# A bidirectional hybrid encoder layer on one core: the first four output blocks computed four rows of input at a time

## The chip, the core and the metric

The kernel runs on one core of a Trainium2 chip. The core has a matrix engine (TensorE, PE in the profile; its weight loads are shown as PEld), a vector engine (VectorE, DVE), a scalar engine (ScalarE, ACT), GpSimd (POOL, unused here but for four constants) and SyncE (SP), whose queue issues almost all transfers from HBM into on-chip memory (SBUF). TensorE writes its sums to PSUM, which here is cut into four accumulators named g and four named s. The metric is the device time of one launch in microseconds (us); the kernel before takes 1975.64 us (median of 3 runs, 1975.63 to 1977.07).

## What is computed

One encoder layer on 256 tokens of width 2048: a root-mean-square norm, one wide projection, a latent attention branch, a two-directional state-space branch, a gated sum, and a feed-forward block. Only the start of it matters here:

```python
n = rms_norm(h, norm_mix_w[l])
u = n @ w_in[l]
q_lat, kv_lat, k_rope, z, xbc, dt_f, dt_b, g_attn, g_ssd = jnp.split(u, IN_SPLITS, axis=-1)
# q_lat and kv_lat are 512 wide each; each is normed again:
q = (rms_norm(q_lat, q_norm_w) @ w_uq)
kv = (rms_norm(kv_lat, kv_norm_w) @ w_ukv)
```

The rest of `u`, the two branches and the feed-forward block follow, and the output is normed once more. All of it is float32.

## The kernel before

**Tiles.** Activations lie transposed: channels on the 128 partitions, the 256 tokens along the row. x is 16 blocks of 128 channels, called k = 0 to 15, and is loaded as four tiles x0 to x3 of four blocks each (512 KB). A weight is cut into blocks of 128 output channels; one such block has 16 sub-blocks of 128x128, one for each k, and is loaded into a tile `raw` (1024 KB). There are three `raw` buffers (`RAWB`).

**Split arithmetic.** A float32 weight w is split into wh (ScalarE copies it to the rounded type fp32r, line 150) and wl = w - wh (VectorE, line 151), eight sub-blocks at a time: a "half". There are five buffers (`HB`) for wh and five for wl, so at most five halves are split ahead. x times the norm's weight is called xw (VectorE, line 275) and is split in the same way into xHL, which holds the high part and the low part side by side (ScalarE line 281, VectorE line 282). One sub-block then costs TensorE two instructions: wh times both parts (512 columns, line 176) and wl times the high part (256 columns, line 177).

**Jobs.** The program is a list of jobs, each one block of outputs: job 0 to 3 give q_lat, 4 to 7 kv_lat, and so on through the layer. Job i takes one accumulator g, runs over its 16 k, and is then evacuated: ScalarE copies one half of g to SBUF and VectorE adds the other (`halves_sum`, lines 228 and 229). An accumulator is free again when both have read it; there are four. For each half that TensorE takes, the loop at the end of the program loads raw tiles and splits halves up to `HB` ahead (`load`, `split_to`).

**The first job.** Job 0 uses no split: it multiplies float32 weights with float32 xw (`first_slab`, line 1143), all 16 k into one accumulator, while the xHL tiles are made.

**Side work.** Slots hang other work on a job: at slot 2 the squares of x (`emit_xsq`: four squares of 1024 columns on ScalarE, three sums of 1024 columns on VectorE and a last one of 512 columns, tiles xsq and xacc), at slot 4 the sums of these over channels on TensorE (line 243, accumulators s).

**What sets the order.** Inside the part marked `manual_schedule` the written order stands. Elsewhere a planner places each engine's instructions by its own costs; an engine then executes its queue strictly in that order. SP's queue issues a transfer only when an earlier transfer on the same one of eight counters has landed.

Of the kernel before, what the change touches and what calls it, by code (L numbers as in the profile page):

```python
# [15 lines left out]
P = 128  # L16
S = 256
# [30 lines left out]
class Job:  # L48


    def __init__(self, src, nb, mm, evac):
        self.src, self.nb, self.mm, self.evac = src, nb, mm, evac
        self.sides, self.post = [], []
        self.whole = None
        self.quad = False


@with_exitstack
def tile_bidir_hybrid_layer(ctx: ExitStack, tc, xT, pos, vec, cst, w_in, w_r, w_v, w_qk, w_oa,
                            w_os, w_out, w_up, w_dn, out, RAWB=3, HB=5, NPG=29, NP1=18):  # L60
    nc = tc.nc
# [7 lines left out]
    act, dve, pe = nc.scalar, nc.vector, nc.tensor  # L69

    def page(shape, dt=F32, name="pg"):
        return pp.tile(shape, dt, tag="pg", bufs=NPG, name=name)

    def p1(shape=(P, S), dt=F32, name="p1"):
        return pp.tile(list(shape), dt, tag="p1", bufs=NP1, name=name)

    def gpsum(shape):
        return gps.tile(shape, F32, tag="g", name="g")

    def spsum(shape):  # L80
        return sps.tile(shape, F32, tag="s", name="s")

    def f32(ap):
        return ap.bitcast(F32)


    V = cp.tile([P, NVEC], F32, name="V")
    CT = cp.tile([P, NCONST], F32, name="CT")
    nc.scalar.dma_start(V[:, :16], vec[:, :16])
    xpg = []  # L90

    def load_x(q):
        t = page([P, 4, S], name=f"x{q}")
        nc.sync.dma_start(t, xT[:, 4 * q:4 * q + 4, :])
        xpg.append(t)
# [6 lines left out]
    def vcol(name, i=0):  # L102
        o = VOFF[name] + i
        return V[:, o:o + 1]
# [4 lines left out]
    jobs = []  # L109
    raws = {}  # L110
    halves = []

    def load(i):
        if i >= len(jobs) or i in raws:
            return
        j = jobs[i]
        t = wp.tile([P, 16, P], F32, tag="raw", bufs=RAWB, name="raw")
        raws[i] = t
        if i == 0:

            for h in range(2):
                load_x(2 * h)
                nc.sync.dma_start(t[:, 8 * h:8 * h + 8, :], j.src[:, 8 * h:8 * h + 8, :])
                load_x(2 * h + 1)
        elif i == 1:
            for h in range(2):
                nc.sync.dma_start(t[:, 8 * h:8 * h + 8, :], j.src[:, 8 * h:8 * h + 8, :])
        elif j.quad:
            tq = t.rearrange("p (m k) c -> p m k c", m=4)
            for m, src in enumerate(j.src):  # L130
                nc.sync.dma_start(tq[:, m], src)
        else:
            nc.sync.dma_start(t[:, :j.nb, :], j.src)
# [4 lines left out]
    def split_to(n):  # L138
        while hptr[0] < min(n, len(halves)):
            i, h, nb = halves[hptr[0]]  # L140
            wh = wp.tile([P, 8, P], F32R, tag="wh", bufs=HB, name="wh")
            wl = wp.tile([P, 8, P], F32R, tag="wl", bufs=HB, name="wl")
            if jobs[i].quad:

                r = raws[i].rearrange("p (m k) c -> p m k c", m=4)[:, :, 2 * h:2 * h + 2, :]
                vh, vl = (w.rearrange("p (k m) c -> p m k c", k=2) for w in (wh, wl))
            else:
                r = raws[i][:, 8 * h:8 * h + nb, :]
                vh, vl = wh[:, :nb, :], wl[:, :nb, :]
            act.activation(vh, r, AF.Copy)  # L150
            dve.tensor_sub(vl, r, f32(vh))  # L151
            hl[hptr[0]] = (wh, wl)
            hptr[0] += 1
# [6 lines left out]
    def dense(src, nb, get, evac, cell=None, k0=0, ktot=None, merge=True):  # L160

        cell = {} if cell is None else cell
        ktot = nb if ktot is None else ktot

        def mm(h, n, wh, wl):
            if k0 == 0 and h == 0:
                cell["ps"] = gpsum([P, 2, S] if merge else [P, S])  # L170
            ps = cell["ps"]
            for b in range(n):
                k = k0 + 8 * h + b
                x = get(k)
                if merge:
                    pe.matmul(ps, lhsT=wh[:, b, :], rhs=x, start=k == 0, stop=False)  # L176
                    pe.matmul(ps[:, 0, :], lhsT=wl[:, b, :], rhs=x[:, 0, :], start=False, stop=k == ktot - 1)  # L177
                else:
                    mm3(ps, wh[:, b, :], wl[:, b, :], x[:, 0, :], x[:, 1, :], k == 0, k == ktot - 1)

        def ev():
            if k0 + nb == ktot:
                evac(cell["ps"])
        j = Job(src, nb, mm, ev)
        jobs.append(j)
        return j
# [40 lines left out]
    def halves_sum(ps, o):  # L227
        act.activation(o, ps[:, 1, :], AF.Copy)
        dve.tensor_add(o, o, ps[:, 0, :])  # L229
# [40 lines left out]
    nHL, xHL, r_x, xw = {}, {}, {}, {}  # L270

    def emit_xw(q):
        xw[q] = page([P, 4, S], name="xw")
        for k in range(4):
            dve.tensor_scalar(xw[q][:, k, :], xpg[q][:, k, :], vcol("nmix", 4 * q + k), None, ALU.mult)

    def emit_split(q, st):
        for b in range(2):
            t = page([P, 2, 2, S], F32R, name="xHL")
            v = xw[q][:, 2 * b:2 * b + 2, :]  # L280
            act.activation(t[:, 0], v, AF.Copy)
            dve.tensor_sub(t[:, 1], v, f32(t[:, 0]))
            st[2 * q + b] = t
# [24 lines left out]
    def pair(st, k):  # L308
        return st[k // 2][:, :, k % 2, :]
# [70 lines left out]
    def lat_evac(which, m):  # L380
        def ev(ps):
            if m == 0:
                lat[which] = page([P, 4, S], name=which)
                lat[which + "s"] = p1(name=which + "s")
            sq = lat[which + "s"] if m == 0 else p1(name="sq1")
            o = lat[which][:, m, :]
            if len(ps.shape) == 2:
                act.activation(o, ps, AF.Copy)
            else:
                halves_sum(ps, o)  # L390
            act.activation(sq, o, AF.Square)
            if m:
                dve.tensor_add(lat[which + "s"], lat[which + "s"], sq)
        return ev
# [565 lines left out]
    win_i = [0]  # L960

    def win(evac, st=nHL, merge=True):
        j = dense(w_in[win_i[0]], 16, lambda k: pair(st, k), evac, merge=merge)
        win_i[0] += 1
        return j
# [3 lines left out]
    def at(slot, fn, *a):  # L969
        late.append((slot, lambda: fn(*a)))  # L970

    for m in range(4):
        win(lat_evac("q", m), xHL, m > 0)
    for m in range(4):
        win(lat_evac("kv", m), xHL, True)
    win(kr_evac)
# [99 lines left out]
    for g in range(G):  # L1076
        b = len(jobs)
# [21 lines left out]
    b = len(jobs)  # L1099
# [4 lines left out]
    b = len(jobs)  # L1104
# [5 lines left out]
    b = len(jobs)  # L1110
# [9 lines left out]
    b = len(jobs)  # L1120
    parts = ((0, 16), (16, 32), (32, 44))
    di = 0
    for pi, (m0, m1) in enumerate(parts):
# [3 lines left out]
        n = m1 - m0  # L1127
# [8 lines left out]
    for s, fn in late:  # L1136
        jobs[s].sides.append(fn)
    base = []

    def first_slab():  # L1140
        ps = gpsum([P, S])
        for k in range(16):
            pe.matmul(ps, lhsT=raws[0][:, k, :], rhs=xw[k // 4][:, k % 4, :], start=k == 0, stop=k == 15)
        return ps
    jobs[0].whole = first_slab
    for i, j in enumerate(jobs):
        base.append(len(halves))
        if j.whole:
# [2 lines left out]
            halves.append((i, h, min(8, j.nb - 8 * h)))  # L1151
    for i in range(RAWB):
        load(i)
    nc.sync.dma_start(CT, cst)
    nc.sync.dma_start(V[:, 16:], vec[:, 16:])

    warm = spsum([P, P])
    for i in range(13):
        pe.matmul(warm, lhsT=ones, rhs=ones, start=True, stop=True)
    with tc.manual_schedule():  # L1160
        emit_xw(0)
        emit_xw(1)
        emit_split(0, xHL)
        emit_xw(2)
        emit_split(1, xHL)
        emit_xw(3)
        emit_split(2, xHL)
        split_to(1)
        emit_split(3, xHL)
        split_to(2)  # L1170
    for i, j in enumerate(jobs):
        load(i + RAWB - 1)
        for fn in j.sides:
            fn()
        if j.whole:
            ps = j.whole()
            raws.pop(i, None)
            lat_evac("q", 0)(ps)
            continue
        for h in range((j.nb + 7) // 8):  # L1180
            n = base[i] + h
            k = halves[min(n + HB - 1, len(halves) - 1)][0]
            for q in range(i, k + 1):
                load(q)
            split_to(n + HB)
            wh, wl = hl.pop(n)
            j.mm(h, halves[n][2], wh, wl)
        raws.pop(i, None)
        for fn in j.post:
            fn()  # L1190
        j.evac()
# [88 lines left out]
```

## Time and profile before

| what | value |
|---|---|
| runs | 1975.63, 1975.64, 1977.07 us; median 1975.64 |
| the profiled execution's own time | 1974.66 us |
| its span, first to last instruction | 1972.9 us |
| granted TensorE clock, mean | 0.998 |
| HBM read | 371.91 MB |

The views used are the page (busy time of each engine), the waits (which engine waited for which line, and for how long), the timeline (single instructions of one engine in order of time), groups of instructions by line, the transfers with their time from issue to landing, and a table by stretches of time (windows), whose columns are busy time and count for each engine, then the granted TensorE clock, the share of time in which the 16 transfer engines were busy, and GB/s. In the timeline a row holds the start, the time, the engine, the line and the tiles, and in brackets the idle time ahead of it and what ended it.

### The profile page before, as it was taken

To read this page: it belongs to the slowest core of one execution; us is meant where nothing else is said; L and a number is where in the kernel's file an instruction comes from. 1 tells how busy PE (TensorE), PEld (TensorE's weight loads), DVE (VectorE), ACT (ScalarE), POOL (GpSimd) and SP (SyncE) were. 2 spreads that over 40 slices of the span, in tenths; PEclk is the share of its full clock that TensorE was granted. 3 is DMA by queue.
4 is the path that set the end of the run, shared out by engine and by line. 5 is a ranking of instruction groups with operands and counts; after the bars stand their busy time and mean duration, and the time that the engine had idled before them with its cause. 6 is when DMAs were issued, how large, how long until landed. Compare 5 with 4: busy or idle time off the path is not lost.

```text
span 1972.9 us, 29057 instructions
## 1 busy us (share of the span) xinstructions
PE 1956.5 (99%) x11136; PEld 1702.4 (86%) x11136; DVE 1466.5 (74%) x2349; ACT 1208.5 (61%) x1892; POOL 0.2 (0%) x4
## 2 busy tenths in 40 slices
PE   9999999999999999999999999999999999999997
PEld 8899988888888888888888888888888888888886
DVE  7997745779887988888455576888657777557776
ACT  6666544688988898786444455555435555345564
POOL 0000000000000000000000000000000000000000
PEclk9999999999999999999999999999999999999999
DMA  7554456666466556645766565555555555555553
GB/s 289 166 175 157 137 180 225 230 214 220 165 215 214 204 180 220 221 158 173 229 198 200 199 219 192 188 188 186 185 192 186 180 190 192 179 185 192 187 161 123
DMA packets 93260, 379.32 MB, mean 192 GB/s; under 512 B 10688, under 2 KB 11328, under 8 KB 62912
## 3 DMA queue, kind: packets, MB, share of 16 engines
q1 hardware_dynamic: 91440, 375.09, 56.2%
q10 hardware_dynamic: 1680, 2.37, 0.4%
q8 instruction: 87, 1.43, 0.3%
q14 instruction: 53, 0.43, 0.1%
HBM read 371.91 MB, written 4.33 MB: 191 GB/s over the span
## 4 chain that ended last, share of the span: by engine, by line
PE 93%; DVE 3%; ACT 2%; issue 1%; DMA 1%; SPq 0%; DVEq 0%; ACTq 0%
PE g L176 41%; PE g L177 21%; PE g L204 7%; PE g L206 7%; PE g L205 7%; PE g L158 1%; PE g L157 1%; PE g L156 1%; DVE wl L151 1%; ACT wh L150 1%; PE s L780 1%; PE s L157 0%; PE s L789 0%; DVE bcf L675 0%; PE s L158 0%
## 5 line engine op out<-in xcount | busy, mean ns | idle before, releaser
L151 DVE TENSOR_TENSOR wl<-raw,wh 128x1024 fp32r<-128x1024 f32 (+1 forms) x670 | 809.3, 1212 | 393.9 <-ACT wh L150 381.5
L150 ACT ACTIVATE wh<-raw 128x1024 fp32r<-128x1024 f32 (+1 forms) x670 | 700.3, 1048 | 647.8 <-PE g L176 433.1
L176 PE MATMUL g<-xHL,wh 128*128 128x512 f32 x1424 | 503.7, 398 | 2.0 <-DVE cu L229 2.0
L176 PE MATMUL g<-hHL,wh 128*128 128x512 f32 x1360 | 477.6, 396 | 0.0
L177 PE MATMUL g<-xHL,wl 128*128 128x256 f32 x1424 | 399.8, 281 | 0.8 <-DVE wl L151 0.8
L177 PE MATMUL g<-hHL,wl 128*128 128x256 f32 x1360 | 381.6, 281 | 0.0
L176 PEld LDWEIGHTS g<-xHL,wh 128*128 128x128 f32 x1424 | 267.3, 188 | 65.7 <-issue 1.2
L176 PEld LDWEIGHTS g<-hHL,wh 128*128 128x128 f32 x1360 | 255.1, 188 | 60.8
L177 PEld LDWEIGHTS g<-xHL,wl 128*128 128x128 f32 x1424 | 269.1, 189 | 1.5 <-DVE wl L151 1.1
L177 PEld LDWEIGHTS g<-hHL,wl 128*128 128x128 f32 x1360 | 257.0, 189 | 0.0
L176 PE MATMUL g<-aHL,wh 128*128 128x512 f32 x692 | 243.7, 398 | 0.0
L177 PE MATMUL g<-aHL,wl 128*128 128x256 f32 x692 | 193.2, 280 | 0.0
L176 PEld LDWEIGHTS g<-aHL,wh 128*128 128x128 f32 x692 | 130.0, 188 | 32.1 <-DVE aHL L919 0.7
L177 PEld LDWEIGHTS g<-aHL,wl 128*128 128x128 f32 x692 | 130.5, 189 | 0.1
L204 PE MATMUL g<-wh,xHL 128*128 128x512 f32 x256 | 100.1, 392 | 0.0
L204 PE MATMUL g<-wh,yHL 128*128 128x512 f32 x256 | 99.8, 390 | 0.0
L206 PE MATMUL g<-wh,xHL 128*128 128x512 f32 x256 | 99.8, 390 | 0.0
L205 PE MATMUL g<-wl,xHL 128*128 128x512 f32 x256 | 99.8, 390 | 0.0
L206 PE MATMUL g<-wh,yHL 128*128 128x512 f32 x256 | 99.6, 389 | 0.0
L205 PE MATMUL g<-wl,yHL 128*128 128x512 f32 x256 | 99.6, 389 | 0.0
L901 DVE SCALAR_TENSOR_TENSOR uc<-u,V,uc 128x255 f32<-128x255 f32 x176 | 84.7, 481 | 4.6 <-ACT uc L899 1.5
L176 PE MATMUL g<-mHL,wh 128*128 128x512 f32 x240 | 83.6, 392 | 0.0
(298 smaller groups left out, 2603.5 us busy)
## 6 DMA issues: line engine op xcount, KB each, us to landing
raw<-in_w_in SPq DMA_DIRECT2D x88, 1024.0 KB, 4.9
raw<-in_w_up SPq DMA_DIRECT2D x88, 1024.0 KB, 4.9
raw<-in_w_in SPq DMA_DIRECT2D x128, 256.0 KB, 4.0
raw<-in_w_os SPq DMA_DIRECT2D x128, 256.0 KB, 3.5
raw<-in_w_dn SPq DMA_DIRECT2D x32, 1024.0 KB, 4.9
raw<-in_w_oa SPq DMA_DIRECT2D x64, 256.0 KB, 3.8
FB<-acsD SPq DMA_DIRECT2D x32, 512.0 KB, 7.5
raw<-in_w_out SPq DMA_DIRECT2D x14, 1024.0 KB, 4.9
```

What stands on the lines that cost most here:

```text
L150: act.activation(vh, r, AF.Copy)
L151: dve.tensor_sub(vl, r, f32(vh))
L156: pe.matmul(ps, lhsT=wH, rhs=xH, start=first, stop=False)
L157: pe.matmul(ps, lhsT=wH, rhs=xL, start=False, stop=False)
L158: pe.matmul(ps, lhsT=wL, rhs=xH, start=False, stop=last)
L176: pe.matmul(ps, lhsT=wh[:, b, :], rhs=x, start=k == 0, stop=False)
L177: pe.matmul(ps[:, 0, :], lhsT=wl[:, b, :], rhs=x[:, 0, :], start=False, stop=k == ktot - 1)
L204: pe.matmul(ps, lhsT=x[:, 0, ts], rhs=wH[:, kk, :], start=k == 0, stop=False)
L205: pe.matmul(ps, lhsT=x[:, 0, ts], rhs=wL[:, kk, :], start=False, stop=False)
L206: pe.matmul(ps, lhsT=x[:, 1, ts], rhs=wH[:, kk, :], start=False, stop=k == kt - 1)
L780: pe.matmul(px[j0][:, b, c * P:(c + 1) * P], lhsT=q.xw[:, 1 - c, js], rhs=q.cX[:, 1 - c, :], start=True, stop=True)
L901: dve.scalar_tensor_tensor(o[:, a], u[:, b], vcol("fcw", k * 88 + cb), o[:, a], ALU.mult, ALU.add)
```

## The change

Jobs 0 to 3 no longer are one output block each. They become four units: unit u holds sub-blocks k = 4u to 4u+3 of all four q_lat blocks. All four accumulators g are taken by unit 0 and are kept until unit 3 is done; then all four are evacuated. Unit 0 (k = 0 to 3) multiplies in float32 without a split; units 1 to 3 use the split. A unit's raw tile is loaded in four pieces of 256 KB (rows of 2 KB in each partition) in place of one or two transfers with rows of 8 or 4 KB. At k = 4 the instruction with wh is issued as two of 256 columns. The tiles x0 to x3 are loaded one ahead of each unit's raw tile, the small tile V (the norm's weights) goes first on SP's queue in place of ScalarE's, the split of x0 is made last, and ten rather than thirteen warm-up matmuls are issued.

```diff
-    nc.scalar.dma_start(V[:, :16], vec[:, :16])
+    nc.sync.dma_start(V[:, :16], vec[:, :16])
...
-        if i == 0:
...
-            for h in range(2):
-                load_x(2 * h)
-                nc.sync.dma_start(t[:, 8 * h:8 * h + 8, :], j.src[:, 8 * h:8 * h + 8, :])
-                load_x(2 * h + 1)
-        elif i == 1:
...
+        if j.four:
...
+            if i < 3:
+                load_x(i)
+            for m, src in enumerate(j.src):
+                nc.sync.dma_start(t[:, 4 * m:4 * m + 4, :], src)
...
-    for m in range(4):
-        win(lat_evac("q", m), xHL, m > 0)
...
+    lps = []
+
+    def first_unit(u):
+        def mm(h, n, wh, wl):
+            for b in range(8):
+                m, k = 2 * h + b // 4, 4 * u + b % 4
+                x = pair(xHL, k)
+                if k == 4:
+                    for i in range(2):
+                        pe.matmul(lps[m][:, i, :], lhsT=wh[:, b, :], rhs=x[:, i, :], start=False, stop=False)
+                else:
+                    pe.matmul(lps[m], lhsT=wh[:, b, :], rhs=x, start=False, stop=False)
+                pe.matmul(lps[m][:, 0, :], lhsT=wl[:, b, :], rhs=x[:, 0, :], start=False, stop=k == 15)
+
+        def whole():
+            for m in range(4):
+                lps.append(gpsum([P, 2, S]))
+                for k in range(4):
+                    pe.matmul(lps[m][:, 0, :], lhsT=raws[0][:, 4 * m + k, :], rhs=xw[0][:, k, :],
+                              start=k == 0, stop=False)
+
+        def ev():
+            if u == 3:
+                for m in range(4):
+                    lat_evac("q", m)(lps[m])
+        j = Job([w_in[m][:, 4 * u:4 * u + 4, :] for m in range(4)], 16, mm, ev)
+        j.four = True
...
+    for u in range(4):
+        jobs.append(first_unit(u))
...
+    load_x(3)
     nc.sync.dma_start(CT, cst)
     nc.sync.dma_start(V[:, 16:], vec[:, 16:])
...
-    for i in range(13):
+    for i in range(10):
         pe.matmul(warm, lhsT=ones, rhs=ones, start=True, stop=True)
     with tc.manual_schedule():
         emit_xw(0)
-        emit_xw(1)
+        for q in (1, 2):
+            emit_xw(q)
+            emit_split(q, xHL)
+            split_to(2 * q)
+        emit_xw(3)
+        emit_split(3, xHL)
         emit_split(0, xHL)
...
```

Three queues show what this moves. Numbers behind a tile's name tell its copies apart. Line numbers of the changed kernel are three lower up to the new function.

**SP's queue, from its start.** Before, the raw tiles of jobs 0 to 3 are raw_89, raw_100, raw_103 and raw_197:

```order
L94 DMA x0_90<-in_xT 128x1024
L123 DMA raw_89<-in_w_in 128x1024
L94 DMA x1_93<-in_xT 128x1024
L94 DMA x2_95<-in_xT 128x1024
L123 DMA raw_89<-in_w_in 128x1024
L94 DMA x3_98<-in_xT 128x1024
L127 DMA raw_100<-in_w_in 128x1024 x2
L133 DMA raw_103<-in_w_in 128x2048
L1154 DMA CT_73<-in_cst 128x386
L1155 DMA V_72<-in_vec 128x746
L133 DMA raw_197<-in_w_in 128x2048
```

Now the raw tiles of units 0 to 3 are raw_89, raw_96, raw_103 and raw_208, and raw_257 and raw_311 belong to the first two kv_lat jobs:

```order
L89 DMA V_72<-in_vec 128x16
L94 DMA x0_90<-in_xT 128x1024
L124 DMA raw_89<-in_w_in 128x512 x4
L94 DMA x1_97<-in_xT 128x1024
L124 DMA raw_96<-in_w_in 128x512 x4
L94 DMA x2_104<-in_xT 128x1024
L124 DMA raw_103<-in_w_in 128x512 x4
L94 DMA x3_110<-in_xT 128x1024
L1179 DMA CT_73<-in_cst 128x386
L1180 DMA V_72<-in_vec 128x746
L124 DMA raw_208<-in_w_in 128x512 x4
```

The same bytes come up to the fourth raw tile. x1 now stands behind all of the first raw tile, not behind half of it, and the fourth raw tile ends behind 16 small pieces.

**ScalarE's queue where the fourth raw tile arrives.** Before, with raw_197 of job 3 split as wh_207 and wh_228:

```order
L287 ACTIVATE xacc_255<-x0_90 128x1024
L290 ACTIVATE xsq_257<-x1_93 128x1024
L150 ACTIVATE wh_207<-raw_197 128x1024
L150 ACTIVATE wh_228<-raw_197 128x1024
L228 ACTIVATE q_193<-g_211 128x256
L290 ACTIVATE xsq_260<-x2_95 128x1024
L290 ACTIVATE xsq_263<-x3_98 128x1024
L391 ACTIVATE sq1_248<-q_193 128x256
L150 ACTIVATE wh_267<-raw_253 128x1024
L150 ACTIVATE wh_288<-raw_253 128x1024
L228 ACTIVATE q_193<-g_271 128x256
```

Now, from the second half of unit 3 (wh_235, from the last two pieces of raw_208) on; wh_271 is the first half of job 4:

```order
L147 ACTIVATE wh_235<-raw_208 128x1024
L278 ACTIVATE xHL_175<-xw_170 128x512
L278 ACTIVATE xHL_178<-xw_170 128x512
L278 ACTIVATE xHL_181<-xw_127 128x512
L278 ACTIVATE xHL_184<-xw_127 128x512
L284 ACTIVATE xacc_259<-x0_90 128x1024
L287 ACTIVATE xsq_261<-x1_97 128x1024
L287 ACTIVATE xsq_264<-x2_104 128x1024
L287 ACTIVATE xsq_267<-x3_110 128x1024
L147 ACTIVATE wh_271<-raw_257 128x1024
L147 ACTIVATE wh_291<-raw_257 128x1024
L147 ACTIVATE wh_313<-raw_311 128x1024
```

All of the splits of x3 and x0 and the four squares now stand between the last half of unit 3 and the first half of job 4.

**VectorE's queue up to the evacuation of the q_lat blocks.** Before, g_211 and g_271 are the accumulators of jobs 1 and 2, wl_268 and wl_289 are the two halves of job 4 (raw_253):

```order
L151 TENSOR_TENSOR wl_208<-raw_197,wh_207 128x1024
L151 TENSOR_TENSOR wl_229<-raw_197,wh_228 128x1024
L229 TENSOR_TENSOR q_193<-q_193,g_211 128x256
L291 TENSOR_TENSOR xacc_255<-xacc_255,xsq_260 128x1024
L393 TENSOR_TENSOR qs_194<-qs_194,sq1_248 128x256
L291 TENSOR_TENSOR xacc_255<-xacc_255,xsq_263 128x1024
L151 TENSOR_TENSOR wl_268<-raw_253,wh_267 128x1024
L292 TENSOR_TENSOR xacc_255<-xacc_255 128x512
L151 TENSOR_TENSOR wl_289<-raw_253,wh_288 128x1024
L229 TENSOR_TENSOR q_193<-q_193,g_271 128x256
L151 TENSOR_TENSOR wl_316<-raw_313,wh_315 128x1024
```

Now g_188, g_193, g_198 and g_203 are the four accumulators of the units, and wl_272 to wl_334 belong to jobs 4 and 5:

```order
L288 TENSOR_TENSOR xacc_259<-xacc_259,xsq_264 128x1024
L148 TENSOR_TENSOR wl_272<-raw_257,wh_271 128x1024
L288 TENSOR_TENSOR xacc_259<-xacc_259,xsq_267 128x1024
L148 TENSOR_TENSOR wl_292<-raw_257,wh_291 128x1024
L289 TENSOR_TENSOR xacc_259<-xacc_259 128x512
L148 TENSOR_TENSOR wl_314<-raw_311,wh_313 128x1024
L148 TENSOR_TENSOR wl_334<-raw_311,wh_333 128x1024
L226 TENSOR_TENSOR q_353<-q_353,g_188 128x256
L226 TENSOR_TENSOR q_353<-q_353,g_193 128x256
L226 TENSOR_TENSOR q_353<-q_353,g_198 128x256
L226 TENSOR_TENSOR q_353<-q_353,g_203 128x256
```

The add that frees an accumulator stood behind the halves of the job being computed, one add for each block; now the first of the four adds stands behind all four halves of jobs 4 and 5. Job 4 takes its accumulator from these four.

More of the change, by code (lines that the diff above doesn't have):

```diff
@@ L54, in __init__ @@
         self.whole = None
-        self.quad = False
+        self.quad = self.four = False
 @with_exitstack
@@ L118, in load @@
         raws[i] = t
-        if i == 0:
-            for h in range(2):
-                load_x(2 * h)
-                nc.sync.dma_start(t[:, 8 * h:8 * h + 8, :], j.src[:, 8 * h:8 * h + 8, :])
-                load_x(2 * h + 1)
-        elif i == 1:
-            for h in range(2):
-                nc.sync.dma_start(t[:, 8 * h:8 * h + 8, :], j.src[:, 8 * h:8 * h + 8, :])
+        if j.four:
[3 more added lines that the diff above has]
+                nc.sync.dma_start(t[:, 4 * m:4 * m + 4, :], src)
         elif j.quad:
@@ L970, in at @@
         late.append((slot, lambda: fn(*a)))
-    for m in range(4):
-        win(lat_evac("q", m), xHL, m > 0)
+    lps = []
[22 more added lines that the diff above has]
+        j.four = True
+        if u == 0:
+            j.whole = whole
+        return j
+    for u in range(4):
+        jobs.append(first_unit(u))
+    win_i[0] += 4
     for m in range(4):
@@ L1138, in tile_bidir_hybrid_layer @@
     base = []
[L1140 to L1145, printed above, removed]
     for i, j in enumerate(jobs):
@@ L1161, in tile_bidir_hybrid_layer @@
         emit_xw(0)
-        emit_xw(1)
-        emit_split(0, xHL)
[L1164 to L1170, printed above, removed]
+        for q in (1, 2):
[4 more added lines that the diff above has]
+        emit_split(3, xHL)
+        emit_split(0, xHL)
     for i, j in enumerate(jobs):
@@ L1175, in tile_bidir_hybrid_layer @@
         if j.whole:
-            ps = j.whole()
+            j.whole()
             raws.pop(i, None)
-            lat_evac("q", 0)(ps)
             continue
```

## The prediction

> **What bounds the kernel now.** I read the page first, then TensorE's waits, then the head in the timeline.
>
> ```profile
> span 1972.9 us, 29057 instructions
> PE 1956.5 (99%) x11136; PEld 1702.4 (86%) x11136; DVE 1466.5 (74%) x2349; ACT 1208.5 (61%) x1892; POOL 0.2 (0%) x4
> ```
>
> TensorE is the bound: 1956.5 of 1972.9 us. The launch ends when its work is done, so only its idle time and its rate can change.
>
> ```profile
> PE g L176 <- DVE cu L229: 2.0, 2, 1.1
> PE s L1159 <- DVE epsc L100: 1.0, 1, 1.0
> PE g L1143 <- DVE xw L275: 1.0, 2, 0.7
> ...
> PE g L177 <- DVE wl L151: 0.8, 1, 0.8
> ```
>
> The longest wait is 1.1 us. Nothing between the first split job and the end has slack in which a delay could vanish: what the head loses or gains moves the end. The head itself:
>
> ```profile
> 7.92 1.14 DVE L275 TENSOR_SCALAR xw<-x,V 128x256 f32<-128x256 f32 x4 [1.24 <-DMA x<-in_xT]
> ...
> 16.04 0.39 PE L177 MATMUL g<-xHL,wl 128*128 128x256 f32 x1 [0.76 <-DVE wl L151]
> ...
> 32.87 0.95 PE L243 MATMUL s<-ones,xacc 128*128 128x1 f32 x8
> 33.68 0.48 PE L176 MATMUL g<-xHL,wh 128*128 128x512 f32 x1
> ```
>
> From 16.04 us TensorE runs without a pause. At 33.68 it begins job 4, the first kv_lat block, with jobs 0 to 3 done. From job 4 on both kernels do the same work in the same order, so I compare the start of job 4.
>
> **The start of job 4 after the change.** The order shows that job 4 needs the accumulator g_188, and VectorE's add that frees it now stands behind wl_272, a sum xacc, wl_292, the last xacc, wl_314 and wl_334. wl_272 needs wh_271, and ScalarE makes that only behind wh_235, four splits and four squares. wh_235 needs the last two pieces of the fourth raw tile. So this is a chain of three terms: landing, ScalarE, VectorE. All three are work that lay beside TensorE before, because each accumulator had been freed long ahead of its next use.
>
> ScalarE and VectorE, in rows that show how closely such instructions follow each other:
>
> ```profile
> 18.72 1.05 ACT L150 ACTIVATE wh<-raw 128x1024 fp32r<-128x1024 f32 x1
> 19.68 1.04 ACT L287 ACTIVATE xacc<-x 128x1024 f32<-128x1024 f32 x1
> ...
> 21.57 1.99 ACT L150 ACTIVATE wh<-raw 128x1024 fp32r<-128x1024 f32 x2
> ...
> 23.73 2.00 ACT L290 ACTIVATE xsq<-x 128x1024 f32<-128x1024 f32 x2
> ...
> 46.92 1.66 ACT L281 ACTIVATE xHL<-xw 128x512 fp32r<-128x512 f32 x3
> ...
> 22.84 2.35 DVE L151 TENSOR_TENSOR wl<-raw,wh 128x1024 fp32r<-128x1024 f32 x2
> 25.11 0.41 DVE L229 TENSOR_TENSOR q<-q,g 128x256 f32<-128x256 f32 x1
> 25.44 1.22 DVE L291 TENSOR_TENSOR xacc<-xacc,xsq 128x1024 f32<-128x1024 f32 x1
> ...
> 29.18 0.69 DVE L292 TENSOR_TENSOR xacc<-xacc 128x512 f32<-128x512 f32 x1
> ```
>
> Two wh take 1.99 us where one takes 1.05, so they follow each other 0.94 apart; squares 0.96 (2.00 less 1.04); three splits of 512 columns take 1.66, or 0.55 each. ScalarE: 0.94 (wh_235) + 4 x 0.55 + 4 x 0.96 + 1.05 (wh_271 in full) = 8.0 us. On VectorE 1024-column instructions stand 1.13 apart (2.35 less 1.22); I take 0.60 for the 512-column one (0.69 less the same 0.09): wl_272, xacc, wl_292, the last xacc, wl_314, wl_334 and the add take 1.13 + 1.13 + 1.13 + 0.60 + 1.13 + 1.13 + 0.41 = 6.7 us. This is 14.7 us from landing to free accumulator.
>
> The landing:
>
> ```profile
> 0.73 0.41 ACTq L89 DMA_DIRECT2D V<-in_vec  x1
> ...
> 14.86 24.54 SPq L133 DMA_DIRECT2D raw<-in_w_in  x7
> ...
> raw<-in_w_in SPq DMA_DIRECT2D x1, 1024.0 KB, 6.5
> ...
> 7.00:9.00 2.00, 2.00 (x11) 1.74 (x10) 1.08 (x5) 0.78 (x2) 0.00 (x0) 1.00 1.04 420
> ...
> ...
> 58.29 1.75 SPq L131 DMA_DIRECT2D raw<-in_w_in  x4
> ...
> 60.00:62.00 2.00, 2.00 (x13) 1.75 (x12) 2.00 (x4) 1.83 (x3) 0.00 (x0) 1.00 0.98 314
> ```
>
> The fourth raw tile is issued at 14.86 and lands 6.5 us later, at 21.4. The bytes up to it are the same after the change and the queue stays full (its issue waits for wl_148, about 15 us, while earlier bytes are still on the way). Two things delay it: V's issue ahead of x0 (0.4 us, the first row), and rows of 2 KB. While 4 KB rows arrive the engines move 420 GB/s (7 to 9 us); while the 2 KB rows of a later unit arrive, issued from 58.29 in four pieces, 314 GB/s at a share of 0.98 (60 to 62 us). 256 KB at these rates are 0.62 and 0.83 us: 0.21 us more for each of 16 pieces, at most 3.4 us. The lower end is nothing, since the slow stretch is one unit's short burst and the head's queue is long. I take the middle, 1.7 us: landing at 21.4 + 0.4 + 1.7 = 23.5, between 21.8 and 25.2. Job 4 starts at 23.5 + 14.7 = 38.2, or 4.5 us later than 33.7.
>
> [...]
>
> **What this costs beyond the wait.** Units 1 to 3 end near 32 us (they start near 14 and hold 48 pairs, and jobs 1 to 3 took 16.0 to 32.9 for the same 48). Then TensorE has some 6 us with only the four small L243 matmuls in them. What such a pause does is seen at the kernel's end:
>
> ```profile
> 1960.51 0.28 PE L158 MATMUL g<-aHL,wl 128*128 128x256 f32 x1
> 1960.63 0.50 PE L243 MATMUL s<-ones,ssf 128*128 128x1 f32 x4
> 1961.76 0.61 PE L243 MATMUL s<-ones,sqf 128*128 128x1 f32 x4 [0.62 <-ACT sqf L940]
> ...
> 1962.00:1964.00 2.00, 1.07 (x8) 0.80 (x7) 0.66 (x4) 0.66 (x3) 0.00 (x0) 1.00 0.00 0
> 1964.00:1966.00 2.00, 0.00 (x0) 0.00 (x0) 2.00 (x4) 0.00 (x0) 0.00 (x0) 0.56 0.21 77
> ```
>
> After the last dense matmul at 1960.5 only a few small ones follow, and by 1964.3 the granted clock is halved (0.56 is the mean of 1964 to 1966). So the pause ahead of job 4 halves it too. What a restart takes is seen at the start, in the warm-up matmuls alone:
>
> ```profile
> 1.00:2.00 1.00, 0.96 (x4) 0.96 (x5) 1.00 0.50 57
> 2.00:3.00 1.00, 1.00 (x7) 1.00 (x6) 1.00 0.44 153
> 3.00:4.00 1.00, 1.00 (x7) 1.00 (x7) 1.00 0.89 321
> 4.00:5.00 1.00, 1.00 (x6) 1.00 (x6) 1.00 0.89 317
> 5.00:6.00 1.00, 1.00 (x10) 0.88 (x8) 1.00 1.03 369
> ```
>
> From 1.04 to 5 us there are 4 to 7 records in each us, then 10: half rate for 3.9 us (the clock column shows no value of its own there). Job 4 would run its first 3.9 us at about half rate and lose 3.9 x 0.47 = 1.85 us. Bounds: nothing, if the clock stays up, and 3.2 us, if the slow phase lasts nearly twice as long.
>
> [...]
>
> **Parts that I cost at nothing.** The float32 unit has the same 16 matmuls as job 0; k = 4 adds four instructions of 256 columns; three warm-up matmuls go; the earlier start of unit 1 (below) gains nothing. All lie ahead of the 6 us pause; if that went, the four instructions would cost about 0.4 us. SP's ten more issues lie on an idle queue. The wait is new for everything behind it on TensorE; ScalarE and VectorE meanwhile split up to five halves ahead, so nothing else is late when job 4 starts.
>
> **Sum.** 4.5 + 1.85 = 6.35 us later. The profiled execution took 1974.66 us (span 1972.9 and 1.8 around it): 1981.0. The median shown is 1.0 us above that execution: 1975.64 + 6.35 = 1982.0.
>
> **Rivals.** 0.2% is 3.95 us, about what a measurement of this kernel can tell from no change.
>
> B, small rows at the slow rate throughout: landing 25.2, job 4 at 39.9, +6.2 and +1.85: 1983.7; with the long slow phase 1985.0. For it: the 314 GB/s row. Against: that queue was short.
>
> C, row size costs nothing: landing 21.8, job 4 at 36.5, +2.8 and +1.85: 1980.3.
>
> D, the clock is not halved: +4.5, 1980.1; with C +2.8, 1978.4, within 0.2%. Against: the tail's row, which was halved after a shorter pause.
>
> E, not slower: x1 lands by 9.9 us (two more 256 KB pieces ahead of it than the 7.92 row shows, and V), the split of x1 and of the first half of unit 1 ends near 14.1, and TensorE starts it 1.9 us ahead of the 16.04 row. If the accumulators were free in time this would stay: 1973.7. That needs the fourth raw tile by 33.7 - 1.9 - 14.7 = 17.1 us, and the same bytes needed 21.4. Only an error in my reading of the queues gives this.
>
> **Chances.** Forecast 0.52 (own range 1980.3 to 1983.7), B 0.16, C 0.14, D 0.13, E 0.05. Slower by over 0.2%: the forecast, B, 0.11 of C and 0.08 of D, together 0.87. The remaining 0.13, E and the rest of C and D, lie within 0.2%, but for 0.02 that I leave for an E larger than worked out: 0.11 and 0.02. The range goes from D with C, 1978.4, to B with the long slow phase, 1985.0; this leaves out E and little else.
>
> **What would show it.** Right: TensorE's longest waits stand ahead of the small s matmuls and job 4's first matmul, ended by VectorE's xacc and q lines, some 6 us in all; the granted clock is near 0.5 in a stretch from about 36 to 41 us; job 4 starts near 38; the fourth raw tile lands near 23.5; later waits are as before. Wrong: job 4 by 34, no drop of the clock, or new waits later in the layer.

## The result and the profile after

The changed kernel takes 1982.12 us (median of 6 runs, 1980.53 to 1983.68) where the kernel before took 1975.64 us beside it (6 runs, 1974.53 to 1977.07). The ratio is 1.0033, 95% interval 1.0023 to 1.0043: slower by a third of a per cent. The profiled execution of the changed kernel took 1981.58 us, 6.9 us more than that of the kernel before.

The page of the changed kernel, its span and busy times:

```profile
span 1979.8 us, 29075 instructions
PE 1959.0 (99%) x11134; PEld 1704.6 (86%) x11134; DVE 1466.8 (74%) x2350; ACT 1208.1 (61%) x1892; POOL 0.2 (0%) x4
```

TensorE is busy 2.5 us longer, although it has two instructions less, and idle 4.4 us longer (20.8 us of its span, 16.4 before). Both parts have to be found. First the idle part: TensorE's waits over the whole run (in total, times, longest).

```profile
PE s L240 <- DVE xacc L289: 3.5, 1, 3.5
PE g L173 <- DVE cu L226: 2.0, 2, 1.0
PE g L989 <- DVE xw L272: 1.4, 1, 1.4
...
PE g L173 <- DVE q L226: 0.8, 1, 0.8
```

The first and the last row are new: one wait for VectorE's last sum of squares (xacc), one for its add that frees an accumulator (q). The rows between stood there before, the xw row with 1.0. Where the two lie, TensorE's timeline of the changed kernel shows, with the first matmul of unit 1 that needs a wl, the last one of unit 3, the small s matmuls and job 4's first:

```profile
14.86 0.39 PE L983 MATMUL g<-xHL,wl 128*128 128x256 f32 x1 [0.76 <-DVE wl L148]
...
31.59 0.28 PE L983 MATMUL g<-xHL,wl 128*128 128x256 f32 x1
35.34 1.86 PE L240 MATMUL s<-ones,xacc 128*128 128x1 f32 x8 [3.47 <-DVE xacc L289]
38.03 0.76 PE L173 MATMUL g<-xHL,wh 128*128 128x512 f32 x1 [0.83 <-DVE q L226]
```

Unit 3 is done at 31.87, a microsecond ahead of the place of job 3 before. Then TensorE does nothing but the small s matmuls for 6.2 us. Job 4 begins at 38.03, where it began at 33.68: 4.35 us later. Its first matmul now takes 0.76 us, not 0.48.

The second part is in the stretches of the changed kernel (busy time and count by engine, granted clock, transfers):

```profile
34.00:36.00 2.00, 0.66 (x4) 0.67 (x4) 2.00 (x3) 2.00 (x5) 0.00 (x0) 0.75 0.42 61
36.00:38.00 2.00, 1.20 (x6) 1.12 (x7) 2.00 (x4) 0.09 (x2) 0.00 (x0) 0.50 0.74 307
38.00:41.00 3.00, 2.97 (x9) 2.61 (x10) 2.68 (x6) 2.97 (x7) 0.00 (x0) 0.50 0.93 287
41.00:42.00 1.00, 1.00 (x5) 0.80 (x5) 0.48 (x2) 0.03 (x1) 0.00 (x0) 0.58 0.87 369
```

The clock is halved from 35.0 (0.75 is the mean of one fast and one slow microsecond) to 41.8 (0.58 is slow for 0.84 of a microsecond; from 42 on it is 1.00). This slow stretch of 6.8 us begins inside the pause and covers the first 3.8 us of job 4.

To see what the head costs in all, I follow one VectorE instruction that stands well behind it, in the attention branch, and which both kernels have. Its row in the kernel before, then in the changed kernel:

```profile
134.34 0.16 DVE L610 TENSOR_SCALAR sm<-sm 128x2 f32<-128x2 f32 x1
...
140.35 0.16 DVE L607 TENSOR_SCALAR sm<-sm 128x2 f32<-128x2 f32 x1
```

It is 6.01 us later: 4.35 from the start of job 4, and 1.66 that job 4 lost at half clock. From there to 1917 us the difference stays between 5.4 and 6.1; over the last 50 us it grows to about 6.9, with no new wait. The runs below lack that late growth or have it in other sizes, and some have a step of 1.4 us between 1098 and 1252 us, again with no wait of TensorE. So I compare experiments by this marked instruction, and by the median only where it can tell.

### The profile page after: what moved, and what is told of

Same layout as the page of the kernel before. It is cut to its first block, busy times and chain, and to the rows that moved or that the text cites. A ratio compares the mean times of both kernels' runs of the same rounds, so it can differ in the third digit from the quotient of the medians.

```text
span 1979.8 us, 29075 instructions
## 1 busy us (share of the span) xinstructions
PE 1959.0 (99%) x11134; PEld 1704.6 (86%) x11134; DVE 1466.8 (74%) x2350; ACT 1208.1 (61%) x1892; POOL 0.2 (0%) x4
## 4 chain that ended last, share of the span: by engine, by line
PE 93%; DVE 3%; ACT 3%; issue 1%; DMA 1%; SPq 0%; DVEq 0%; ACTq 0%
PE g L173 40%; PE g L174 20%; PE g L201 7%; PE g L203 7%; PE g L202 7%; PE g L155 1%; PE g L154 1%; PE g L153 1%; DVE wl L148 1%; ACT wh L147 1%; PE s L777 0%; PE s L154 0%; DVE bcf L672 0%; PE s L786 0%; PE s L155 0%
## 5 line engine op out<-in xcount | busy, mean ns | idle before, releaser
L173 PE MATMUL g<-xHL,wh 128*128 128x512 f32 x1376 | 488.0, 398 | 2.8 <-DVE cu L226 2.0
L174 PE MATMUL g<-xHL,wl 128*128 128x256 f32 x1376 | 386.8, 281 | 0.0
L173 PEld LDWEIGHTS g<-xHL,wh 128*128 128x128 f32 x1376 | 259.1, 188 | 64.2 <-PE s L155 2.3
L174 PEld LDWEIGHTS g<-xHL,wl 128*128 128x128 f32 x1376 | 260.8, 190 | 0.4
```

## The experiments

All lateness below is that of the marked instruction against 134.34 us. The ratios of e1, e2, e3 and e5 are to the kernel before at 1976.33 us (17 runs, 1975.21 to 1977.36), those of e4, e7, e8 and e9 to 1974.93 us (24 runs, 1974.13 to 1976.59), as each was measured beside it.

| kernel | unit 3's end to job 4, largest waits | clock halved | job 4 begins | marked instruction late by | median, ratio (95%) |
|---|---|---|---|---|---|
| changed kernel | 3.5, 0.8 | 35.0 to 41.8 | 38.03 | 6.01 | 1982.12, 1.0033 (1.0023 to 1.0043) |
| e8_filled2 | 0.6 | never | 37.35 | 4.62 | 1981.12, 1.0030 (1.0019 to 1.0041) |
| e3_filled | 3.1 | 35.9 to 42.7 | 40.94 | 7.95 | 1983.71, 1.0035 (1.0022 to 1.0047) |
| e1_other_acc | 3.8 | 37.0 to 40.5 | 36.85 | 4.70 | 1982.45, 1.0029 (1.0017 to 1.0041) |
| e5_sums_later | 3.6, 1.4 | 36.0 to 42.8 | 38.00 | 8.45 | 1984.33, 1.0040 (1.0025 to 1.0055) |
| e2_acc_and_sums | none | never | 31.72 | 3.04 | 1979.64, 1.0020 (1.0011 to 1.0030) |
| e7_squares_later | 0.2 | 44.1 to 47.5 | 32.47 | 5.82 | 1980.02, 1.0028 (1.0017 to 1.0038) |
| e4_rows4k | 1.0, 1.6 | 38.1 to 41.5 | 36.92 | 4.71 | 1980.31, 1.0024 (1.0014 to 1.0034) |
| e9_repaired | none | never | 31.57 | 1.68 | 1977.97, 1.0017 (1.0008 to 1.0026) |

### What the lower clock costs: the pause filled with work

e3_filled puts small matmuls with constant operands ahead of and behind the s matmuls; nothing uses their sums.

```diff
+    def keep(n):
+        ps = spsum([P, P])
+        for _ in range(n):
+            pe.matmul(ps, lhsT=ones, rhs=ones, start=True, stop=True)
+
+    at(4, keep, 15)
     at(4, emit_xr)
+    at(4, keep, 8)
```

> The changed kernel with matmuls of ones, whose result nobody reads, put into the pause: 15 ahead of the four small matmuls and 8 behind them (added work, nothing else is changed). Theory: job 4 starts where it did, 38.0 to 38.6, since it waits for VectorE and not for TensorE; but the granted clock stays at 1.00 through job 4, which saves the 1.75 us that half rate cost from 38.0 to 41.8: near 1980.4. Rival (the clock is no part of the loss): the same time as the changed kernel or, with the added work, up to 0.5 us more.

It told nothing: the first fifteen depend on nothing and were placed at the kernel's start, so the pause stayed open. The other eight ran behind it at half clock (0.50 from 36 to 41 us), on the path. TensorE's timeline of e3_filled (16 records for eight float32 matmuls, as for the s matmuls):

```profile
37.52 3.76 PE L1013 MATMUL s<-ones 128*128 128x128 f32 x16
```

e8_filled2 does it again with fillers that read unit 3's last wl, so that they can't be placed earlier:

```diff
         def ev():
             if u == 3:
+                fill = spsum([P, 512])
+                for i in range(22):
+                    pe.matmul(fill, lhsT=last[0][:, 0, :], rhs=last[0][:, 0:4, :], start=True, stop=True)
```

> 22 matmuls more, each 128x128 by 128x512 in bf16, read the last rounding of the first unit's weights, stand on TensorE between that unit and the small s matmuls, and their sums are used by nothing: extra work put into the pause, at full rate about 5 us long. Theory (the pause itself costs 4.4 us, and 1.7 us come on top because TensorE's clock is halved after it): the fillers run from 31.7 to about 36.7, the granted clock stays at 1.00, the first kv_lat block starts at 38.0 to 38.4 as without them, and work near 134 us is 4.2 to 4.6 us later than in the kernel before, where the changed kernel's is 6.0 later. Rival (the clock falls for another reason, or its fall costs nothing): the clock is at 0.50 behind the fillers as well, or it stays up and the shift is 5.5 or more.

(The tile wl is not bf16, as the expectation has it, but fp32r.) TensorE's timeline of e8_filled2 between unit 3 and job 4, and the stretch behind job 4's start:

```profile
30.85 5.16 PE L1000 MATMUL s<-wl 128*128 128x512 f32 x22
35.85 0.95 PE L240 MATMUL s<-ones,xacc 128*128 128x1 f32 x8
37.35 0.47 PE L173 MATMUL g<-xHL,wh 128*128 128x512 f32 x1 [0.55 <-DVE q L226]
```

```profile
38.00:41.00 3.00, 3.00 (x19) 2.66 (x18) 2.69 (x6) 2.97 (x6) 0.00 (x0) 1.00 0.98 360
```

Five microseconds of useless work in the pause delayed nothing in job 4 and kept the clock at 1.00: 19 matmuls between 38 and 41 us where the changed kernel has 9. From the start of job 4 (3.67 us late; its fourth raw tile came 0.7 us earlier than in the changed kernel) the lateness falls a little, to 3.55 near 90 us, where in the changed kernel it grows from 4.35 to 6.0 in the same job. That settles the clock's share: 1.66 us in the changed kernel, none here. The marked instruction is 4.62 late as expected, but for another reason than the sum says: 1.05 us of that came in this run some 105 us from the start, where TensorE waits for wl for 0.4 and 0.9 us (0.6 once in the kernel before).

### What holds job 4: two waits, one behind the other

Three edits, of which the third is the first two together. e1_other_acc gives the first kv_lat block an accumulator of the s group, which is free:

```diff
-        win(lat_evac("kv", m), xHL, True)
+        win(lat_evac("kv", m), xHL, True, acc=gpsum if m else spsum)
```

> Job 4 alone takes its accumulator from the four s ones, so that it doesn't wait for the add that frees g_188; the four small matmuls over xacc still stand ahead of it. Theory (two waits stand one behind the other, then the clock): TensorE still idles 3.5 us ahead of the small matmuls, which wait for the last xacc, but the second wait (0.8 us, and the 1.0 us of small matmuls stretched ahead of it) is gone: job 4 starts near 36.3 instead of 38.0, and the clock is still halved, since the pause is still over 4 us. About 1.8 us less than the changed kernel: near 1980.3. Rival (the accumulators are the whole of the wait): job 4 starts near 32.5, the clock stays up, near 1974.5.

e5_sums_later leaves the accumulators alone and moves the small s matmuls and what follows them one slot later:

```diff
-    at(4, emit_xr)
-    at(5, emit_xr2)
+    at(5, emit_xr)
+    at(6, emit_xr2)
```

> The sums over channels of the squares and what follows from them are hung one slot later each (slots 5 and 6 instead of 4 and 5), so that job 4's matmuls no longer stand behind them. Theory: job 4 still waits for the add that frees g_188, starts near 38, the clock is halved: no gain, 1981 to 1984, perhaps 1 us more from what is now late. Rival (the sums are the whole of the wait): job 4 starts near 32.5, near 1974.5.

e2_acc_and_sums has both edits.

> Both edits: job 4 takes an s accumulator, and the sums come one slot later. Theory: neither wait is left, job 4 starts between 31.5 and 33, the pause is about 1 us, and the granted clock stays at 1.00. Up to job 5 this is 5.5 us and, with the clock, 7.3 us less than the changed kernel; the later sums make two waits of 1 to 2 us near 50 and 66 us, so that 1976 to 1979 is left at the end. Rival (the time is lost elsewhere than at job 4): within 1 us of the changed kernel's 1982.1.

TensorE's timelines, first e1_other_acc, then e5_sums_later, then e2_acc_and_sums:

```profile
35.94 1.05 PE L240 MATMUL s<-ones,xacc 128*128 128x1 f32 x8 [3.85 <-DVE xacc L289]
36.85 0.61 PE L173 MATMUL s<-xHL,wh 128*128 128x512 f32 x1
```

```profile
35.31 1.25 PE L240 MATMUL s<-ones,xacc 128*128 128x1 f32 x8 [3.60 <-DVE xacc L289]
38.00 0.77 PE L173 MATMUL g<-xHL,wh 128*128 128x512 f32 x1 [1.45 <-DVE q L226]
```

```profile
31.72 0.39 PE L173 MATMUL s<-xHL,wh 128*128 128x512 f32 x1
32.30 0.38 PE L174 MATMUL s<-xHL,wl 128*128 128x256 f32 x1 [0.19 <-DVE wl L148]
...
37.73 0.95 PE L240 MATMUL s<-ones,xacc 128*128 128x1 f32 x8
```

With another accumulator the q wait is gone, and job 4 follows right behind the small s matmuls, which still wait for xacc: 1.2 us won. The expected gain was 1.8, and 0.6 of it is missing because the fourth raw tile came later in this run (ScalarE began its second half at 23.87 us, against 23.26 in the changed kernel). The median, 1982.45, doesn't show the gain. In e5 the small matmuls still stand ahead of job 4 and wait for xacc, so this edit did not take that wait away as it was meant to; job 4 waits for q behind them and begins at 38.00, as in the changed kernel. Behind that it loses more: 4.8 us of job 4 lie at half clock, and two waits for VectorE, 1.0 us for xHL and 0.6 for latL, are new. With both edits job 4 follows unit 3 at 31.72 and the clock never drops. So the wait for squares and the wait for the accumulator are two, and one has to remove both. That the first by itself holds job 4 nearly as long as both, e1 shows. That the second would too, no run shows by itself; I read it from VectorE's rows of the changed kernel (shown further down), which follow each other without a pause from 31.18 to the adds at 37.47, so that nothing in them waits for the small matmuls.

But job 4's start, now 2.0 us ahead of the kernel before, becomes a lateness of 3.0 at the marked instruction: 5.0 us are lost on the way. The small s matmuls, which now lie behind the start of job 4, are 0.95 of that. TensorE's waits of e2_acc_and_sums from 20 to 140 us give most of the rest, since only the last of these rows has its like in the kernel before:

```profile
PE s L257 <- DVE dg L256: 1.7, 1, 1.7
PE g L173 <- DVE xHL L279: 1.0, 1, 1.0
PE g L154 <- DVE latL L413: 0.6, 1, 0.6
PE g L155 <- DVE wl L148: 0.6, 1, 0.6
```

These are 3.3 us more than before; 0.7 us I can't place. VectorE's work that was done in the pause now stands beside the jobs that follow and is waited for there. The median, 1979.64, lies a little above the expected 1976 to 1979.

### The squares moved instead

e7_squares_later moves the squares themselves, and their sums, behind the release of the accumulators, which stay as they are.

```diff
-    at(2, emit_xsq)
-    at(4, emit_xr)
-    at(5, emit_xr2)
+    at(4, emit_xsq)
+    at(5, emit_xr)
+    at(6, emit_xr2)
```

> ScalarE's squares and VectorE's two sums of them come later in the stream of preparing steps (from slots 2, 3 and 4 to 4, 5 and 6); the accumulators are given out as in the changed kernel. Theory (the pause is the chain of squares, first sum, small s matmuls, accumulator): the first kv_lat block starts at 32.2 to 33.0, with a wait of about 1 us for VectorE's q line, the clock stays at 1.00, and the small s matmuls wait 2 to 3 us near 42 instead. Against the kernel before, later work (near 134 us) is 2 to 4 us later, where the changed kernel's is 6.0 later. Rival (what holds the block is the landing of the fourth raw tile, whatever the order of steps): the block starts at 36 or later and the shift stays at 5.5 to 6.5.

TensorE's timeline of e7_squares_later, and two of its stretches:

```profile
32.47 0.50 PE L173 MATMUL g<-xHL,wh 128*128 128x512 f32 x1 [0.20 <-DVE q L226]
...
42.32 1.05 PE L240 MATMUL s<-ones,xacc 128*128 128x1 f32 x8 [2.42 <-DVE xacc L289]
```

```profile
43.00:45.00 2.00, 2.00 (x12) 1.82 (x12) 1.99 (x4) 0.61 (x3) 0.00 (x0) 0.78 0.27 53
...
44.00:48.00 4.00, 4.00 (x15) 3.43 (x14) 2.22 (x2) 1.36 (x2) 0.00 (x0) 0.57 0.82 287
```

The start of job 4 agrees with the theory: with the squares out of the way the same accumulator from the same add is free 5.6 us earlier, though the fourth raw tile landed no earlier (ScalarE began its second half at 23.43 us, against 23.26 in the changed kernel). So the squares and their sums are what made the add late. The lateness does not agree: 5.82, which is the rival's number for another reason. The s matmuls wait for xacc from 39.9 on; behind this pause of 2.4 us the clock was halved from 44.1 to 47.5 (0.57 is the mean of 44 to 48). Moved, the same chain cost nearly as much in another place.

### The size of the rows

e4_rows4k regroups the first four blocks of w_in in memory, so that each unit's raw tile comes as two transfers of 512 KB with rows of 4 KB. The computation is the same.

```diff
-            for m, src in enumerate(j.src):
-                nc.sync.dma_start(t[:, 4 * m:4 * m + 4, :], src)
+            for h in range(2):
+                nc.sync.dma_start(t[:, 8 * h:8 * h + 8, :], j.src[:, 8 * h:8 * h + 8, :])
...
+    a["w_in"][:4] = a["w_in"][:4].reshape(4, P, 4, 4, P).transpose(2, 1, 0, 3, 4).reshape(4, P, 16, P)
```

> The first four blocks of w_in lie in memory in another order, so that each raw tile of the first unit comes as two transfers of 512 KB with rows of 4 KB, where the changed kernel has four of 256 KB with rows of 2 KB. Nothing else is changed. Theory of the prediction (row size costs 1.7 us by the fourth raw tile): the last piece lands at 21.5 to 22.0 where the changed kernel has 23.16, and the first kv_lat block starts near 36.6 where it has 38.03. Rival, by the landings of the changed kernel (in a full queue its 2 KB pieces land 0.66 to 0.67 apart, and most of the delay is two breaks of 0.6 us between 7 and 12 us): the last piece lands at 22.5 to 23.0 and the block starts at 37.3 to 37.9. By both the clock is still halved after the pause, for one or two stretches of 3.41 us.

ScalarE's timeline shows the landing of the fourth raw tile, as wh of each half begins when its pieces are there. First the changed kernel, then e4_rows4k:

```profile
21.93 1.06 ACT L147 ACTIVATE wh<-raw 128x1024 fp32r<-128x1024 f32 x1 [2.23 <-DMA raw<-in_w_in]
23.26 1.06 ACT L147 ACTIVATE wh<-raw 128x1024 fp32r<-128x1024 f32 x1 [0.27 <-DMA raw<-in_w_in]
24.22 2.18 ACT L278 ACTIVATE xHL<-xw 128x512 fp32r<-128x512 f32 x4
26.31 1.05 ACT L284 ACTIVATE xacc<-x 128x1024 f32<-128x1024 f32 x1
27.26 2.94 ACT L287 ACTIVATE xsq<-x 128x1024 f32<-128x1024 f32 x3
30.10 2.94 ACT L147 ACTIVATE wh<-raw 128x1024 fp32r<-128x1024 f32 x3
```

```profile
22.15 1.06 ACT L147 ACTIVATE wh<-raw 128x1024 fp32r<-128x1024 f32 x1 [0.30 <-DMA raw<-in_w_in]
```

The last piece is there 1.1 us earlier, and job 4 begins 1.1 us earlier (36.92): a microsecond of landing is a microsecond of job 4. The transfer rates of both, the last column of these stretches, first the changed kernel, then e4_rows4k:

```profile
7.00:10.00 3.00, 3.00 (x16) 2.64 (x15) 0.00 (x0) 0.00 (x0) 0.00 (x0) 1.00 1.02 343
...
13.00:18.00 5.00, 4.23 (x25) 3.35 (x24) 4.59 (x9) 2.96 (x5) 0.00 (x0) 1.00 1.04 397
```

```profile
7.00:10.00 3.00, 2.49 (x6) 2.05 (x7) 0.01 (x1) 0.00 (x0) 0.00 (x0) 0.56 1.04 400
...
13.00:18.00 5.00, 5.00 (x29) 4.48 (x28) 4.64 (x9) 2.99 (x5) 0.00 (x0) 1.00 1.03 407
```

The small pieces cost 2 to 3% from 13 us on (397 and 407 GB/s), but 14% between 7 and 10 us (343 against 400), where they come with breaks: the second and third of the first raw tile land at 6.96 and 8.15 us, while later ones land 0.67 apart. (In e4 the first matmul waits 2.6 us for its larger piece, and the clock, 0.56 from 7 to 10 us, was halved there once more; unit 3 ended at 33.2 us, which the pause ahead of job 4 hides.) Neither expectation is quite met: the landing is at the late end of the theory's window and well ahead of the rival's. Other runs with 2 KB rows scatter (ScalarE began that half between about 22.6 and 23.9 us), so 1.1 us is good to about half a microsecond; e9 below, which has the 4 KB rows too, began it at 22.18, so both runs with them are ahead of all seven without. The edit doubles the rows and halves the number of transfers at once, so which of the two counts stays open.

### All of it together

e9_repaired has the free accumulator of e1, the rows of e4, the squares' sums and VectorE's dg lines one slot later, and the rope's steps spread over six slots.

```diff
-        win(lat_evac("kv", m), xHL, True)
+        win(lat_evac("kv", m), xHL, True, acc=gpsum if m else spsum)
...
-    at(4, emit_xr)
-    at(5, emit_xr2)
+    at(5, emit_xr)
+    at(5, emit_dg)
+    at(6, emit_xr2)
...
-    for m in range(5, 14):
-        at(m, rope_steps, 4 if m < 13 else 99)
+    for m in range(8, 14):
+        at(m, rope_steps, 7 if m < 13 else 99)
```

> The changed kernel with what the runs so far point to: the first kv_lat block takes an accumulator of the s group, the sums of squares and VectorE's dg lines come later, the rope's steps are spread over six slots, and the first unit's raw tiles come with rows of 4 KB (the first four blocks of w_in lie in memory in another order). Theory (the loss was the pause ahead of the first kv_lat block, and the early start of the first unit is worth 1 to 2 us once nothing takes it back): the block starts at 31.5 to 32.5, no wait of TensorE over 1 us from there to 134 us, the clock at 1.00, work near 134 us 1 to 2 us earlier than in the kernel before, and the time 1974 to 1976, same as the kernel before or just below. Rival (taking x as it arrives costs something of its own in the stages behind, as VectorE and ScalarE do the preparing beside the first jobs): other waits of 2 us or more in sum near 40 to 70 us, shift at 134 us +1 to +4, time 1977 to 1980.

TensorE's waits of e9_repaired from 20 to 140 us, and the marked instruction:

```profile
PE g L155 <- DVE wl L148: 1.1, 1, 1.1
PE g L173 <- DVE xHL L279: 0.9, 1, 0.9
PE g L570 <- DVE wl L148: 0.7, 1, 0.7
PE g L571 <- DVE latL L421: 0.2, 1, 0.2
```

```profile
136.02 0.16 DVE L615 TENSOR_SCALAR sm<-sm 128x2 f32<-128x2 f32 x1
```

Up to job 4 the theory is right: it begins at 31.57, 2.1 us ahead of the kernel before, with the clock at 1.00. Behind that the rival is right: late by 1.68, 1977.97 us. Of the 3.8 us lost again, 0.95 are the small s matmuls that now stand behind job 4's start. The waits are 2.9 us where the kernel before has 0.6 in this part, which makes 2.3. About half a microsecond I can't place. This version wins back about half of what the change lost, and no version that I ran beats the kernel before.

## Why the prediction was right

The forecast, 1982.0 us, and the measured 1982.1 agree, and so does the mechanism. Step by step:

**The sum.** Forecast +4.5 for the start of job 4 and +1.85 for the clock; measured 4.35 and 1.66, 6.0 in place of 6.35. The profiled executions differ by 6.9; the last 0.9 of it came mostly in the final 50 us and is no part of the change that any run could show. So the agreement to 0.1 us in the median is luck; that of the first term is not, and that of the second is in part.

**The landing, 23.5.** The second half began at 23.26, so some 0.3 us sooner. The row-size term was 1.7 us and measured 1.1, and what is left when the rows are 4 KB, 22.0, is 0.6 later than before where I had 0.4. One rate for the whole queue was the wrong picture: I priced a slow rate for all 16 pieces, while most of the loss came early, with the breaks: the changed kernel moved 343 GB/s from 7 to 10 us and 363 from 10 to 13, where e4 moved 400 and 408; from 13 to 18 it was 397 against 407. Rivals B and C, the two ends of this term, both fall: 22.15 of e4 against 23.26 excludes C's nothing, and 397 GB/s in the full queue excludes B's 314 throughout.

**The chains, 14.7 us.** ScalarE's rows above go from 23.26 through four splits and four squares to wh at 30.10 (then three in a row), and VectorE's of the changed kernel go on from there:

```profile
31.18 1.23 DVE L148 TENSOR_TENSOR wl<-raw,wh 128x1024 fp32r<-128x1024 f32 x1 [0.21 <-ACT wh L147]
32.33 1.22 DVE L288 TENSOR_TENSOR xacc<-xacc,xsq 128x1024 f32<-128x1024 f32 x1
33.46 1.22 DVE L148 TENSOR_TENSOR wl<-raw,wh 128x1024 fp32r<-128x1024 f32 x1
34.60 0.68 DVE L289 TENSOR_TENSOR xacc<-xacc 128x512 f32<-128x512 f32 x1
35.20 2.35 DVE L148 TENSOR_TENSOR wl<-raw,wh 128x1024 fp32r<-128x1024 f32 x2
37.47 1.40 DVE L226 TENSOR_TENSOR q<-q,g 128x256 f32<-128x256 f32 x4
```

The first of the four adds is done at about 37.9, 14.6 us behind 23.26. This is the step that carried the forecast, and it was read from the order with durations of the trace alone.

**The clock.** Rival D falls: the clock was halved, from 35.0 to 41.8, and e8 shows that keeping it up removes the 1.66 us. I had the slow phase as 3.9 us of job 4; it was 3.8. That is in part luck: in e5, where job 4 begins at 38.00 as well, 4.8 us of it were slow. And the 0.47 by which I multiplied stands in no row that I showed (4 to 7 records against 10 are a loss of 0.3 to 0.6); the runs gave 0.43. No run shows the 3.2 us that I had as the upper bound of this loss and, in B's 1985.0, for the long slow phase. The slow stretches were 3.4 us long in e1, e4 and e7 and 6.8 us in the changed kernel, e3 and e5, and at most 4.8 us of one lay in job 4 (e5).

**Rival E, not slower.** It needed the accumulators in time, and they came too late. Its head start of 1.9 us was too large besides: the first matmul with a wl stands at 14.86, where it stood at 16.04, and unit 3 ends 1.0 us ahead of job 3 before. In e2 job 4 begins 2.0 us ahead, but 0.8 of that is only that the small s matmuls (32.87 to 33.68 before) no longer stand in front of it, so its likeness to the 1.9 is luck. A hundred microseconds on, e2 is late by 3.0. In no run without the pause does the change gain.

**Parts costed at nothing.** "Later waits are as before" holds in the changed kernel, as I read it, because its pause lets VectorE catch up; that reason is argued. As a statement about the change it is wrong: e2 and e9 find 2.3 us and more there as soon as the pause is gone. I also had x1 by 9.9 us, and VectorE's first use of it, which waits for the transfer, began at 10.80; this lay off the path here. And the two waits sum to 4.3 us, not "some 6": the pause is 6.2 us long, but 1.86 of it count as busy with the small matmuls, which at half clock took that long (0.95 before).

## What to carry to other kernels

Work done earlier only helps if what is needed next is free earlier too: here four accumulators that were freed one by one all became free at the end, behind a queue of unrelated preparing work. Read such a queue in the changed order from the last landing to the release, with durations of the old trace; it gave 14.7 us within 0.1. With TensorE 99% busy, the side work taken out of the pause came back here as waits in the next jobs (3.3 us in e2, 2.3 in e9), so price it there; and where a pause can't be avoided, look for half clock behind it and add that loss too, here 0.43 of the slow time (1.66 us for 3.8).

## What the runs showed of the hardware that I had not expected

**Half clock came after short pauses too.** In e7 TensorE idled for 2.4 us, then ran the s matmuls (one column wide) for 1.05 us and matmuls of 256 and 512 columns from 43.24 on; from 44.1 the clock was halved all the same. In e4 it was halved from 38.1, behind pauses of 1.0 and 1.6 us with the s matmuls (1.05 us) between them, although job 4's matmuls had run for 1.2 us by then. It was not halved behind the 0.55 us of e8 (1.00 up to 48 us), nor behind the 1.9 us ahead of the first matmul of the first unit in e9 (1.00 from 7 to 18 us), where e4, with 2.6 us there, has 0.56 from 7 to 10. What decides it, no run shows.

**Half clock cost less than half.** 3.8 us at half clock cost 1.66 us in the changed kernel, and 3.4 us in e4 cost 1.47 (3.24 late at job 4, 4.71 at the marked instruction): 0.43 of the slow time. Job 4's pairs of matmuls nearly agree: one took 0.64 us at half clock and 0.35 before, a loss of 0.45. Why it is not half stays open.

**Useless work was free here.** 22 dense matmuls in the pause made the kernel no slower, delayed nothing in job 4 and kept its clock up (1.00 from 30 to 48 us). The median doesn't show what that saved (ratio 1.0030 against 1.0033).
